# A hybrid attention block with a seven-product MLP: first pieces of a second product prepared behind the last evictions, and VectorE in the source's order

## The chip, the cores and the metric

The kernel runs on one NeuronCore of a Trainium2 chip. The metric is the device time in microseconds (us) of one execution. A core has five engines that run their own instruction streams side by side: TensorE (PE; its weight loads are listed as PEld), VectorE (DVE), ScalarE (ACT), GpSimd (POOL) and SyncE (SP), which here only issues DMA transfers. Each engine takes its instructions strictly in the order in which they stand in its stream, so an instruction that waits holds up everything behind it on the same engine. TensorE accumulates into PSUM banks; the other engines read those ("evict" them) and write to SBUF.

## The reference

One layer of a streaming encoder, 1024 tokens by 1024 features, all in float32:

```
n = rms_norm(x, g1);  proj = n @ w_in
y = [mixer_a(...) , mixer_b(...)]        # two attention groups, each normalised
h = x + concat(y) @ w_out
m = rms_norm(h, g2)
h = h + (relu(m @ w_ff1) ** 2) @ w_ff2   # 1024 -> 4096 -> 1024
out = rms_norm(h, final_g)
```

The change touches the MLP's two products and the work around them, the last third of the time.

## The kernel before, in words

**Seven products for eight.** Both MLP products are done by a Strassen-like scheme: a product of 2x2 blocks of 512 by 512 takes seven block products, with sums and differences of blocks as operands, and each block product takes three TensorE passes over float16 halves (a high part and the rest, the low part). An operand is thus first a float32 tile, then a high part (ScalarE copies it to float16, L1410) and a low part (tile minus high part: GpSimd L1412, or VectorE L1414).

**First product.** The 4096 hidden features come in eight slices n = 0..7. For each slice `product1(n, p)` runs p = 1, 5, 6, 3, 7, 2, 4 (list `order1`); 24 matmuls of 128x512 each. Products 1, 6, 7 and 4 accumulate in one PSUM pair (in the order's names `f1_n_1`), products 5 and 3 in a second, product 2 in a third, so TensorE can begin product 4 only when product 7 has been evicted. ScalarE evicts products 1, 5 and 6 to tiles k; VectorE evicts products 3, 7 and 2 (a custom operation at L1473 adds the PSUM pair to a k tile and takes a row maximum into `topf`, then L1475 squares the positive part). For product 4, ScalarE does relu and square, VectorE a row maximum (L1471), and then come four block sums on VectorE (L1484 to L1490). Every finished block goes by `put` to DRAM (`ud`), seven per slice, on SP's queue in order.

**Second product.** The slices go in four groups g of GQ = 2. `order2` lists pieces (g, p, n): for each product p both slices n of the group accumulate in one pair of PSUM tiles (chain a, b or c). A piece is 24 matmuls. `prepare2(at)` makes the operands of piece `at`, AHEAD2 = 2 pieces ahead of use: U is the block that `load2u` has read back from `ud` (LOAD2 = 6 pieces ahead, SP queue), scaled by ScalarE (L1408) and split (ScalarE L1410, GpSimd L1412; for p = 5 VectorE instead of GpSimd); V is a block of the second weights or a difference Z of such blocks (VectorE L1384), split by ScalarE L1410 and VectorE L1414. After both slices of a product, `add_up` (VectorE, L1733) adds the PSUM tiles to result blocks C, once per half and in some products for two blocks.

The first four pieces, group 0's products 1 and 5, are prepared inside the loop of the first product:

```
FIRST_PIECES = {(7, 1): 0, (7, 5): 1, (7, 6): 2, (7, 3): 3}
...
        if (n, p) in FIRST_PIECES:
            prepare2(FIRST_PIECES[n, p])
```

**The end.** In the last group the order of products is 1, 2, 5, 6, 3, 7, 4. Token blocks 0 to 3 are complete after product 3; their final norms (`final`, generators that are stepped) are issued behind product 7: squares on ScalarE (L1747), small columns and reciprocals on VectorE (L1777, L1779), the scaling on GpSimd and VectorE, and the copy of the gains (L1825). Product 4, which finishes blocks 4 to 7, runs in row pieces (`last_product`), each followed by the norm of its block.

**What sets the order.** A scheduler with a timeline of its own orders each engine's instructions; source order is only its input. The class `InOrder` (L159) wraps an engine so that each of its instructions depends on the one before it in the source, which pins the order; such an instruction has L159 as its line. In the kernel before, SP's queue is pinned in the MLP, ScalarE is pinned in the first product from its ninth step on, TensorE is pinned throughout, and VectorE and ScalarE are pinned in the last product. `dve` is the plain VectorE (L508).

Of the kernel before, what the change touches and what calls it, by code (L numbers as in the profile page):

```python
# [13 lines left out]
ALU = mybir.AluOpType  # L14
# [10 lines left out]
NQ = DFF // (4 * P)  # L25
# [9 lines left out]
GQ = 2  # L35
# [10 lines left out]
}  # L46
FIRST_PIECES = {(7, 1): 0, (7, 5): 1, (7, 6): 2, (7, 3): 3}
START_FILL = 3
A_FILL = 7
B_FILL = [13, 13, 9.5, 9.5] * 2 + [11.25] * 8  # L50
# [15 lines left out]
def kernel(  # L66
# [29 lines left out]
    nc = tc.nc  # L96
# [411 lines left out]
    dve, pool = nc.vector, nc.gpsimd  # L508
# [630 lines left out]
    def flat(t):  # L1139
        return t.rearrange("p a b -> p (a b)")  # L1140
# [278 lines left out]
    def prepare1(n, p, at):  # L1419
        if n >= NQ or (n, p) in wops:  # L1420
            return
        made = wsum.setdefault(n, {})
        if n:
            scaled1(n, *{1: ((0, 0), (0, 1)), 5: ((0, 1), (1, 1)), 6: ((1, 1), (1, 0))}.get(p, ((1, 0), (0, 1), (1, 1))))
        second = page2 if at < 2 or at > 4 else page1
        t = second_operands(
            lambda i, j: w1s[n, i, j], made, p, f"T{n}_{p}", dve, lambda name: second([P, 4, 2 * P], name)
        )
        wops[n, p] = split(
            t, f"W{n}_{p}", dve if at < 7 and at != 2 else pool, lambda name: page16([P, 2, 4, 2 * P], name), None if n else to_scale1[0][0]  # L1430
        )
# [3 lines left out]
    def product1(n, p):  # L1435
        a, c = chains.setdefault(n, [None, None])
        if p in (1, 5, 2):
            ps = pair_psum(f"f1_{n}_{p}")
            if p == 1:
                chains[n][0] = ps  # L1440
            if p == 5:
                chains[n][1] = ps
        else:
            ps = c if p == 3 else a
        hi, lo = wops.pop((n, p))
        for u in range(2):
            cols = slice(u * P, (u + 1) * P)
            for k in range(4):
                x2 = [X[p][k // 2][:, hl, k % 2] for hl in range(2)]
                mm3(ps[:, u], (hi[:, k, cols], lo[:, k, cols]), x2, k == 0 and p in (1, 5, 2), k == 3, True)  # L1450
                if k % 2:
                    turn()
        while stores:
            stores.pop(0)()
        kept = saved.setdefault(n, {})
        ps = flat(ps)
        if p in (1, 5, 6):
            if p == 5 and n:
                kept[p] = tst([P, 2 * HALF], f"k{n}_{p}")
            else:  # L1460
                kept[p] = page2([P, 2 * HALF], f"k{n}_{p}")
            act1[0].activation(kept[p], ps, AF.Copy)
            return
        v = tst([P, 2 * HALF], f"v{n}") if p == 4 else kept[{3: 6, 7: 5, 2: 1}[p]]
        if n not in topf:
            topf[n] = small.tile([P, 4], F32, tag="topf", bufs=2, name=f"topf_{n}")
        top = topf[n][:, {3: 0, 7: 1, 2: 2, 4: 3}[p] :][:, :1]
        if p == 4:
            act1[0].activation(v, ps, AF.Relu)
            act1[0].activation(v, v, AF.Square)  # L1470
            dve.tensor_reduce(top, ps, mybir.AxisListType.X, ALU.max)  # L1471
        else:
            dve.tensor_tensor_reduce(v, ps, v, 1.0, 0.0, ALU.add, ALU.max, top)  # L1473
            if n:
                dve.scalar_tensor_tensor(v, v, 0.0, v, ALU.max, ALU.mult)  # L1475
            else:
                act1[0].activation(v, v, AF.Relu)
                act1[0].activation(v, v, AF.Square)
        if p != 4:
            put(n, {3: 2, 7: 4, 2: 1}[p], v)  # L1480
            return

        u00, u01, u11, u10 = kept[1], kept[6], kept[5], v
        dve.tensor_tensor(u11, u10, u11, ALU.add)  # L1484
        put(n, 5, u11)
        dve.tensor_tensor(u10, u00, u10, ALU.subtract)
        put(n, 7, u10)
        dve.tensor_tensor(u00, u11, u00, ALU.subtract)
        put(n, 6, u00)
        dve.tensor_tensor(u01, u01, u00, ALU.subtract)  # L1490
        put(n, 3, u01)
        if n % GQ == 0:
            topu[n // GQ] = Top(f"u{n // GQ}", NQ + n // GQ, GQ)
        top, col = topf.pop(n), topu[n // GQ].column()
        nc.vector.tensor_reduce(col, top, mybir.AxisListType.X, ALU.max)
        nc.vector.tensor_tensor(col, col, down1[n], ALU.mult)
        if n % GQ == GQ - 1:
            topu[n // GQ].gather()
# [138 lines left out]
    def prepare2(at):  # L1637
        if at >= len(order2) or order2[at][1:] in ready2:
            return
        g, p, n = order2[at]  # L1640
        ready2.add((p, n))
        alloc = page if at <= 3 * GQ else page3
        high = lambda name: page16([P, 2, 2, HALF], name, alloc)
        temp = lambda name: alloc([P, 2, HALF], name, F32)
        a = u2s.pop((n, p))
        b = second_operands(lambda i, j: w2s[n, i, j], made_b.setdefault(n, {}), p, f"Z{n}_{p}", dve, temp)
        ops2[n, p] = (
            split(a, f"U{n}_{p}", dve if p == 5 else pool, high, uup[n]), split(b, f"V{n}_{p}", dve, high, up2[g])
        )

    queue[0] = InOrder(nc.sync)
    for at, (n, p) in enumerate(order1):
        if at == 8:
            act1[0] = InOrder(nc.scalar)
        if p == (1 if n > 1 else 5) and n:
            load1(n + 1)
        ahead1 = at + (AHEAD1 + 1 if at < AT_ONCE else AHEAD1)

        behind = (n, p) == (0, 2)
        if ahead1 < len(order1) and not behind:  # L1660
            prepare1(*order1[ahead1], ahead1)
        product1(n, p)
        for work in chores.get((n, p), ()):
            combined(*work)
            if behind and work[0] == 5:
                prepare1(*order1[ahead1], ahead1)
        if 0 < n < NQ - 1:
            if p == 3:
                see1(n + 1)
            if p == 7:  # L1670
                scale1(n + 1)
        if p == 3 and n and n % GQ == 0:
            scale_of_u(n // GQ - 1)
        if at > 6:
            look2(at, p != 1)
        for i, blocks in FIRST_LOADS.get((n, p), ()):
            if i is not None:
                fetch2(i)
            for tile2 in blocks:
                load2w(*tile2)  # L1680
        if (n, p) in FIRST_PIECES:
            prepare2(FIRST_PIECES[n, p])
    assert not to_see and not on_way and not to_scale
    act1[0] = nc.scalar
    acc = {}
# [44 lines left out]
    def add_up(p, q2):  # L1730
        ps = banks["a" if p in (1, 6, 7, 4) else "b" if p == 2 else "c"][q2]
        c = acc[(*into[p], q2)]
        nc.vector.scalar_tensor_tensor(flat(c), flat(ps), down2[g], flat(c), ALU.mult, ALU.add)  # L1733

    def final(tb, dve, act, first=None):

# [64 lines left out]
    for at, (g, p, n) in enumerate(order2[:-GQ]):  # L1801
        fetch2(at + LOAD2)
        step = at % (7 * GQ)
        if g + 1 < NQ // GQ:
            if step in range(4, 12):
                load2w(*blocks2(g + 1)[step - 4])
        if step == 1:
            scale_sums(g)
        if g + 1 == NQ // GQ and step == 2:
            down, up = down2[g], scale_tile("up", "", 1)  # L1810
            nc.vector.reciprocal(up, down)
        if g == 0 and step in (4, 7, 10):
            last = NQ // GQ - 1
            {4: topu[last].write, 7: topu[last].read, 10: lambda: scale_of_u(last, False)}[step]()
        prepare2(at + AHEAD2)
        if at in (1, 3, 9):
            load_acc(*into[{1: 5, 3: 6, 9: 4}[at]])
        if at == 6:
            queue[0].dma_start(gfb, final_g.partition_broadcast(P))
        if product2(g, p, n):  # L1820
            for q2 in range(2):
                add_up(p, q2)
        if (g, p) == (NQ // GQ - 1, 3) and n % GQ == GQ - 1:
            gains.append(fps.tile([P, D], F32, tag=f"{'ab'[1 ^ g % 2]}0", bufs=1, name="gains"))
            nc.scalar.activation(gains[0], gfb, AF.Copy)  # L1825
        if (g, p) == (NQ // GQ - 1, 7):
            if n % GQ == GQ - 1:
                h = acc[1, 0, 1][:, 1]
                nc.vector.scalar_tensor_tensor(h, banks["a"][1][:, 1], down, h, ALU.mult, ALU.add)
            two = [final(2 * (n % GQ) + b, dve, nc.scalar) for b in range(2)]  # L1830
            for _ in range(4):
                for work in two:
                    next(work)

    g, p, n0 = order2[-GQ]
    in_order = InOrder(nc.vector), InOrder(nc.scalar)

# [102 lines left out]
```

## Time and profile before

| what | value |
|---|---|
| three runs | 1033.74, 1030.7, 1032.37 us; median 1032.37 |
| the profiled execution: its own time | 1034.48 us |
| the profiled execution: span from first to last instruction | 1032.7 us |
| mean granted TensorE clock | 0.994 |
| DMA moved | 200.63 MB, mean 194 GB/s |
| U tiles read back from `ud` | 56 transfers of 512 KB, median 5.7 us from issue to landing |
| results stored to `ud` | 48 transfers of 512 KB in that group, 3.6 us |

Times in the views are microseconds from the start of the span. In a timeline a row is: start, busy time, engine, line, operation, out<-in, partitions x elements and type, count, and in brackets the idle time ahead of it on that engine and what ended it. A wait row is: engine, what waits, line, `<-` what released it, then total us, times, longest. In the rows of windows: the stretch, its length, then busy time (and instructions) of PE, PEld, DVE, ACT and POOL, the granted TensorE clock, the busy share of DMA and GB/s. Busy shares are averages over stages with different limits, and the profiled execution is 2.1 us above the median of the three runs, so differences are taken against its own span.

### The profile page before, as it was taken

How to read it: one execution, taken by the hardware profiler on the slowest of the kernel's cores; microseconds unless marked ns; L12 is line 12 of the kernel's file. 1: busy time of each engine (PE TensorE's matmuls, PEld its weight loads, DVE VectorE, ACT ScalarE, POOL GpSimd, SP SyncE). 2: the span in 40 equal slices, each digit the busy share in tenths (PEclk: the TensorE clock that was granted, in tenths of full speed). 3: DMA queues.
4: the chain of work that ended last, by engine and by line, in shares of the span. 5: the costliest groups of instructions: out<-in, count | busy, mean ns of one | idle time of the engine just before them, and what ended most of it. 6: DMA issues, size and time to landing. Idle time of an engine off the chain costs nothing. (4 is left out here: it accounts for less than half of the span.)

```text
span 1032.7 us, 14046 instructions
## 1 busy us (share of the span) xinstructions
PE 997.6 (97%) x4818; PEld 590.7 (57%) x4818; DVE 805.6 (78%) x1288; ACT 650.5 (63%) x1060; POOL 448.9 (43%) x341
## 2 busy tenths in 40 slices
PE   9999999999979999989999999999899999999997
PEld 7888887777756668644444444444344444444443
DVE  5576787867675738995989999979886887686976
ACT  8676766766576745676646655756286655557446
POOL 0466665242452472106335444446163243345333
PEclk9999999999989999999999999999999999999999
DMA  9944527999999894205778668738699454443004
GB/s 355 267 126 130 139 77 186 192 211 228 211 248 225 201 304 159 86 21 183 252 257 285 218 228 288 248 141 304 223 299 401 142 181 137 169 162 123 1 1 163
DMA packets 150567, 200.63 MB, mean 194 GB/s; under 512 B 78688, under 2 KB 96224, under 8 KB 150496
## 3 DMA queue, kind: packets, MB, share of 16 engines
q1 hardware_dynamic: 150352, 199.47, 64.0%
q8 instruction: 38, 0.62, 0.3%
q14 instruction: 33, 0.27, 0.1%
q10 hardware_dynamic: 144, 0.26, 0.1%
HBM read 120.01 MB, written 42.99 MB: 158 GB/s over the span
## 5 line engine op out<-in xcount | busy, mean ns | idle before, releaser
L179 PE MATMUL f<-X,W 128*128 128x512 f16 x1344 | 294.5, 381 | 6.2 <-DVE topf L1473 3.9
L179 PEld LDWEIGHTS <-W 128*128 128x128 f16 x1344 | 131.6, 98 | 164.0 <-issue 7.5
L179 PEld LDWEIGHTS <-U 128*128 128x128 f16 x1356 | 132.4, 98 | 160.6 <-ACT V L1410 1.8
L1412 POOL TENSOR_TENSOR U<-u,U 128x1024 f16<-128x1024 f32 x48 | 120.9, 2531 | 167.7 <-ACT U L1410 157.3
L179 PE MATMUL f_a<-V,U 128*128 128x512 f16 x756 | 165.3, 379 | 0.9 <-DVE C L1733 0.9
L1412 POOL TENSOR_TENSOR W<-T,W 128x1024 f16<-128x1024 f32 x29 | 73.4, 2532 | 82.6 <-ACT W L159 49.4
L1412 POOL TENSOR_TENSOR W<-w,W 128x1024 f16<-128x1024 f32 x21 | 49.4, 2353 | 90.1 <-ACT W L159 69.2
L1408 ACT ACTIVATE u<-u,uupn 128x1024 f32<-128x1024 f32 x46 | 52.1, 1144 | 56.2 <-DMA u<-ud 55.3
L179 PE MATMUL f_c<-V,U 128*128 128x512 f16 x384 | 84.2, 379 | 1.4 <-DVE C L1733 1.4
L1414 DVE SCALAR_TENSOR_TENSOR V<-Z,up,V 128x1024 f16<-128x1024 f32 x32 | 52.3, 1638 | 28.2 <-ACT V L1410 23.3
L631 ACT ACTIVATE P_B<-P_B,nm_B 128x640 f32<-128x640 f32 (+2 forms) x64 | 44.2, 691 | 32.0 <-DVE nm_B L628 16.5
L1410 ACT ACTIVATE U<-u 128x1024 f16<-128x1024 f32 x46 | 48.1, 1045 | 25.6 <-DVE Z L1384 11.3
L179 PE MATMUL op_A<-w_o,y 128*128 128x512 f32 x192 | 58.6, 430 | 5.7 <-DVE ts_vB L441 5.1
L876 DVE SCALAR_TENSOR_TENSOR H_B<-P_B,rc_B,H_B 128x640 f16<-128x640 f32 (+2 forms) x64 | 50.8, 822 | 13.7 <-ACT H_B L871 13.3
L179 PE MATMUL ip_qB<-nT,w_qB 128*128 128x512 f32 x192 | 53.8, 406 | 1.1 <-DVE t_kB L415 1.0
L1414 DVE SCALAR_TENSOR_TENSOR V<-w,up,V 128x1024 f16<-128x1024 f32 x24 | 42.9, 1791 | 14.8 <-ACT V L1410 7.8
L179 PE MATMUL ip_kB<-nT,w_kB 128*128 128x512 f32 x192 | 53.7, 405 | 0.0
L179 PE MATMUL ip_vB<-nT,w_vB 128*128 128x512 f32 x192 | 51.3, 400 | 0.0
L159 ACT ACTIVATE w<-w,up 128x1024 f32<-128x1024 f32 x24 | 26.7, 1137 | 38.5 <-DVE up L1162 38.5
L179 PE MATMUL ip_qA<-nT,w_qA 128*128 128x512 f32 x192 | 50.5, 397 | 0.3 <-DVE VA L185 0.3
L1410 ACT ACTIVATE V<-Z,up 128x1024 f16<-128x1024 f32 x30 | 34.1, 1137 | 25.4 <-DVE Z L1384 24.8
L871 ACT ACTIVATE H_B<-P_B,rc_B 128x640 f16<-128x640 f32 (+2 forms) x64 | 40.8, 685 | 9.9 <-DVE rc_B L868 4.5
(295 smaller groups left out, 2007.1 us busy)
## 6 DMA issues: line engine op xcount, KB each, us to landing
w<-in_w_ff_dram SPq DMA_DIRECT2D x64, 512.0 KB, 7.2
u<-ud SPq DMA_DIRECT2D x56, 512.0 KB, 5.7
ud<-k SPq DMA_DIRECT2D x48, 512.0 KB, 3.6
m<-in_w_ff_dram SPq DMA_DIRECT2D x32, 512.0 KB, 5.9
KkB<-t_kB SPq DMA_DIRECT2D x32, 256.0 KB, 5.1
xr<-in_x_dram SPq DMA_DIRECT2D x8, 512.0 KB, 9.2
st_o<-in_w_out_dram SPq DMA_DIRECT2D x8, 512.0 KB, 4.3
h<-in_x_dram SPq DMA_DIRECT2D x8, 512.0 KB, 4.9
```

The lines of the kernel that those rows point to most:

```text
L159: ins = getattr(self.engine, op)(*args, **kw)
L179: pe(nc.tensor.matmul(*args, **kw))
L631: nc.scalar.activation(pr, pr, AF.Exp, bias=nm, scale=-1.0, accum_out=sm)
L871: nc.scalar.activation(hi, q, AF.Copy, scale=rc)
L876: nc.vector.scalar_tensor_tensor(lo, q, rc, hi, ALU.mult, ALU.subtract)
L1408: act1[0].activation(full, full, AF.Copy, scale=up)
L1410: act1[0].activation(w[0], full, AF.Copy, scale=1.0 if up is None else up)
L1412: engine.tensor_tensor(w[1], full, w[0], ALU.subtract)
L1414: engine.scalar_tensor_tensor(w[1], full, up, w[0], ALU.mult, ALU.subtract)
```

## The change

Pieces 2 and 3 (group 0's product 5) are prepared two products later in the source, behind the evictions of products 2 and 4 of slice 7. The sums that end slice 7 move into a function `finish1`, called behind the last of these pieces. From product 7 of slice 7 until the last product, `dve` is an `InOrder` VectorE, and `add_up` goes through it. The final norms of blocks 0 to 3 use the plain VectorE as before (they were passed `dve` and are now passed `nc.vector`).

```
-FIRST_PIECES = {(7, 1): 0, (7, 5): 1, (7, 6): 2, (7, 3): 3}
+FIRST_PIECES = {(7, 1): 0, (7, 5): 1, (7, 2): 2, (7, 4): 3}
@@ product1
+        last_sums.append(lambda: finish1(n, kept, v))
+        if n < NQ - 1:
+            last_sums.pop()()
+
+    last_sums = []
+
+    def finish1(n, kept, v):
+
         u00, u01, u11, u10 = kept[1], kept[6], kept[5], v
         dve.tensor_tensor(u11, u10, u11, ALU.add)
@@ loop over order1
+        if (n, p) == (NQ - 1, 7):
+            dve = InOrder(nc.vector)
         product1(n, p)
...
         if (n, p) in FIRST_PIECES:
             prepare2(FIRST_PIECES[n, p])
+        if (n, p) == (NQ - 1, 4):
+            last_sums.pop()()
@@ add_up
-        nc.vector.scalar_tensor_tensor(flat(c), flat(ps), down2[g], flat(c), ALU.mult, ALU.add)
+        dve.scalar_tensor_tensor(flat(c), flat(ps), down2[g], flat(c), ALU.mult, ALU.add)
@@ loop over order2
-            two = [final(2 * (n % GQ) + b, dve, nc.scalar) for b in range(2)]
+            two = [final(2 * (n % GQ) + b, nc.vector, nc.scalar) for b in range(2)]
...
+    dve = nc.vector
     g, p, n0 = order2[-GQ]
     in_order = InOrder(nc.vector), InOrder(nc.scalar)
```

The orders of TensorE and SP stay as they were. Those of VectorE, ScalarE and GpSimd move, at three places above all. In the rows, `k7_5` is the tile that product 7 of slice 7 is evicted to, `k7_6` that of product 3, `k7_1` that of product 2; `Z0_5` or `U1_5` are operands of slice 0's or 1's product 5.

VectorE at the end of the first product, before:

```order
L1384 TENSOR_TENSOR Z0_5_7053<-w2_0_01_6946,w2_0_00_6901 128x1024
L1414 SCALAR_TENSOR_TENSOR V1_1_7013<-w2_1_00_6905,up2_0_5795,V1_1_7013 128x1024
L1384 TENSOR_TENSOR Z1_5_7091<-w2_1_01_6950,w2_1_00_6905 128x1024
L1414 SCALAR_TENSOR_TENSOR U0_5_7055<-u0_5_6944,uupn_0_5570,U0_5_7055 128x1024
L1473 ISA k7_6_7045,topf_7_7088<-f1_7_5_6962,k7_6_7045 128x1024
L1473 ISA topf_7_7088 128x1
L1414 SCALAR_TENSOR_TENSOR V0_5_7058<-Z0_5_7053,up2_0_5795,V0_5_7058 128x1024
L1475 SCALAR_TENSOR_TENSOR k7_6_7045<-k7_6_7045 128x1024
L1414 SCALAR_TENSOR_TENSOR U1_5_7093<-u1_5_6948,uupn_1_5572,U1_5_7093 128x1024
L1414 SCALAR_TENSOR_TENSOR V1_5_7096<-Z1_5_7091,up2_0_5795,V1_5_7096 128x1024
L1473 ISA k7_5_6987,topf_7_7088<-f1_7_1_6913,k7_5_6987 128x1024
```

and the same place now:

```order
L1414 SCALAR_TENSOR_TENSOR V1_1_7013<-w2_1_00_6905,up2_0_5795,V1_1_7013 128x1024
L1473 ISA k7_6_7045,topf_7_7080<-f1_7_5_6962,k7_6_7045 128x1024
L1473 ISA topf_7_7080 128x1
L1475 SCALAR_TENSOR_TENSOR k7_6_7045<-k7_6_7045 128x1024
L159 ISA k7_5_6987,topf_7_7080<-f1_7_1_6913,k7_5_6987 128x1024
L159 ISA topf_7_7080 128x1
L159 SCALAR_TENSOR_TENSOR k7_5_6987<-k7_5_6987 128x1024
L159 ISA k7_1_6942,topf_7_7080<-f1_7_2_7115,k7_1_6942 128x1024
L159 ISA topf_7_7080 128x1
L159 SCALAR_TENSOR_TENSOR k7_1_6942<-k7_1_6942 128x1024
L159 TENSOR_TENSOR Z0_5_7143<-w2_0_01_6946,w2_0_00_6901 128x1024
L159 SCALAR_TENSOR_TENSOR U0_5_7145<-u0_5_6944,uupn_0_5570,U0_5_7145 128x1024
```

The six operations of product 5 (Z, U, V of slices 0 and 1) stood ahead of the eviction of product 7 and now stand behind those of products 7 and 2; behind them come V0_5, the row maximum of product 4, Z1_5, U1_5, V1_5 and then the four sums. On ScalarE, the high parts for product 5 stood ahead of those of the weights of products 2 and 4 of slice 7 and now stand behind them.

ScalarE at group 0's product 7, where `u0_7` is a U tile to be scaled and `U0_7` its high part, before:

```order
L1408 ACTIVATE u0_7_7277<-u0_7_7277,uupn_0_5570 128x1024
L1408 ACTIVATE u1_7_7312<-u1_7_7312,uupn_1_5572 128x1024
L1410 ACTIVATE U0_7_7432<-u0_7_7277 128x1024
L1410 ACTIVATE V0_7_7436<-Z0_7_7430,up2_0_5795 128x1024
L1410 ACTIVATE U1_7_7472<-u1_7_7312 128x1024
L1410 ACTIVATE V1_7_7476<-Z1_7_7470,up2_0_5795 128x1024
L1408 ACTIVATE u0_2_7353<-u0_2_7353,uupn_0_5570 128x1024
L1408 ACTIVATE u1_2_7389<-u1_2_7389,uupn_1_5572 128x1024
```

and now:

```order
L1408 ACTIVATE u0_7_7277<-u0_7_7277,uupn_0_5570 128x1024
L1408 ACTIVATE u1_7_7312<-u1_7_7312,uupn_1_5572 128x1024
L1408 ACTIVATE u0_2_7353<-u0_2_7353,uupn_0_5570 128x1024
L1408 ACTIVATE u1_2_7389<-u1_2_7389,uupn_1_5572 128x1024
L1408 ACTIVATE u0_4_7426<-u0_4_7426,uupn_0_5570 128x1024
L1410 ACTIVATE U0_7_7432<-u0_7_7277 128x1024
L1410 ACTIVATE V0_7_7436<-Z0_7_7430,up2_0_5795 128x1024
L1410 ACTIVATE U1_7_7472<-u1_7_7312 128x1024
```

Three scalings of later products' tiles, u0_4's the last of them, have moved ahead of product 7's high parts; u0_4 stood behind the high parts of product 2.

VectorE ahead of the last product, where `C010` and `C011` are halves of the result block that product 3 completes, `qf`, `wf`, `rf` and `fo` belong to the norms of token blocks 0 to 3, and `V7_4` is an operand of the last product, before:

```order
L1384 TENSOR_TENSOR Z7_4_9203<-w2_7_10_8663,Z7_6_8953 128x1024
L1414 SCALAR_TENSOR_TENSOR V6_4_9132<-Z6_4_9126,up2_3_6999,V6_4_9132 128x1024
L1414 SCALAR_TENSOR_TENSOR V7_4_9209<-Z7_4_9203,up2_3_6999,V7_4_9209 128x1024
L1733 SCALAR_TENSOR_TENSOR C010_7323<-f2_3_c_0_8925,down2_3_8805,C010_7323 128x1024
L1733 SCALAR_TENSOR_TENSOR C011_7325<-f2_3_c_1_8926,down2_3_8805,C011_7325 128x1024
```

and now:

```order
L1789 RECIPROCAL qf_3_9253<-uf_3_9251 128x1
L1791 RECIPROCAL rf_0_9163<-wf_0_9161 128x1
L1790 TENSOR_SCALAR wf_2_9241<-wf_2_9241,qf_2_9242,uf_2_9240 128x1
L1791 RECIPROCAL rf_1_9174<-wf_1_9172 128x1
L1790 TENSOR_SCALAR wf_3_9252<-wf_3_9252,qf_3_9253,uf_3_9251 128x1
L1799 SCALAR_TENSOR_TENSOR fo_0_9159<-C000_7196,rf_0_9163,gains_9124 128x512
L1791 RECIPROCAL rf_2_9243<-wf_2_9241 128x1
L1799 SCALAR_TENSOR_TENSOR fo_1_9170<-C000_7196,rf_1_9174,gains_9124 128x512
L1791 RECIPROCAL rf_3_9254<-wf_3_9252 128x1
L159 SCALAR_TENSOR_TENSOR V7_4_9209<-Z7_4_9203,up2_3_6999,V7_4_9209 128x1024
L159 SCALAR_TENSOR_TENSOR C110_7247<-f2_3_a_0_8777,down2_3_8805,C110_7247 128x1024
```

V7_4 stood ahead of C010 and of all the norms of blocks 0 to 3, and now stands behind their reciprocals; C010 and C011 (rows of product 3) stand ahead of Z6_4 and V6_4 now, where they stood behind V7_4. On ScalarE the squares of the norms, which stood behind the high parts of U and V for the last product, are now mixed in between these high parts.

At one more place, between products 2 and 5 of the last group, VectorE had the additions of product 2 to C000 and C001 behind Z7_6, V6_6 and V7_6 (operands of product 6); they now stand directly behind V7_5.

## The prediction

> **What bounds the kernel now.** The page's first two lines say where to look.
>
> ```profile
> span 1032.7 us, 14046 instructions
> PE 997.6 (97%) x4818; PEld 590.7 (57%) x4818; DVE 805.6 (78%) x1288; ACT 650.5 (63%) x1060; POOL 448.9 (43%) x341
> ```
>
> TensorE is busy for 97% of the span and the change adds no matmul, so only two things can move the time: TensorE's idle gaps and the clock behind a gap. Next, TensorE's waits from 700 us on, all four of them, and the rows of its timeline where they lie.
>
> ```profile
> PE f L179 <- DVE topf L1473: 3.9, 1, 3.9
> PE f L179 <- POOL W L1412: 1.7, 1, 1.7
> PE f_c L179 <- DVE C L1733: 1.4, 1, 1.4
> PE f_a L179 <- DVE C L1733: 0.9, 1, 0.9
> ```
>
> ```profile
> 717.99 4.92 PE L179 MATMUL f<-X,W 128*128 128x512 f16 x22 [1.74 <-POOL W L1412]
> ...
> 726.81 6.91 PE L179 MATMUL f<-X,W 128*128 128x512 f16 x24 [3.90 <-DVE topf L1473]
> 733.56 10.52 PE L179 MATMUL f_a<-V,U 128*128 128x512 f16 x48
> ...
> 775.00 10.52 PE L179 MATMUL f_a<-V,U 128*128 128x512 f16 x48
> ...
> 1004.45 10.52 PE L179 MATMUL f_a<-V,U 128*128 128x512 f16 x48
> 1015.93 7.93 PE L179 MATMUL f_a<-V,U 128*128 128x512 f16 x36 [0.95 <-DVE C L1733]
> ```
>
> The row at 726.81 is slice 7's product 4. 24 matmuls took 6.91 us there; at the rate of the rows of 48 (10.52) they take 5.18 from start to start, so 1.73 us were lost. A window shows why (the number before the last two is the granted clock):
>
> ```profile
> 726.80:730.20 3.40, 3.39 (x9) 1.23 (x9) 3.37 (x4) 0.00 (x0) 0.00 (x0) 0.53 0.38 154
> ```
>
> After 3.90 us idle the clock stood at 0.53 for 3.4 us. The rows at 775.00 (group 0's product 7) and 1004.45 (the last group's product 7) have no gap now.
>
> **Step 1, the end of the first product: a gain.** Why the two gaps ahead of 733.56 exist is in the other engines' timelines:
>
> ```profile
> 714.38 1.04 ACT L159 ACTIVATE W<-w 128x1024 f16<-128x1024 f32 x1
> 715.50 2.43 POOL L1412 TENSOR_TENSOR W<-w,W 128x1024 f16<-128x1024 f32 x1 [5.79 <-ACT W L159]
> 725.54 1.21 DVE L1473 CUSTOM_DVE_ANT_0 k<-f,k 128x1024 f32<-128x1024 f32 x1
> ```
>
> Product 2's weight was split late, since ScalarE's high part (714.38) stood behind product 5's; now product 5's stand behind it, and the 1.74 go. The eviction of product 7 ran at 725.54, although product 7 had ended before 717.99: the six operations for product 5 that stood around it on VectorE ran first, without a pause, as VectorE's own window shows (busy 11.00 of 11.00 us; the clock behind 1.74 us idle stayed at 1.00):
>
> ```profile
> 715.00:726.00 11.00, 11.00 (x9) 1.00 0.72 280
> ```
>
> Now none stands ahead of it. It lies beside product 2's 5.18 us, so the 3.90 go, and with the gap the slow clock, 1.73. Sum −7.37: the second product would start at 726.19 instead of 733.56. What hides the moved operations is the first pieces of group 0: product 1 runs 10.36 us ahead of product 5. Bounds: −7.4, and −5.6 if the weight of product 2 is no earlier (it also waits for GpSimd); I take −7.37, because nothing is left on ScalarE ahead of it.
>
> **Step 2, group 0's product 7: a new wait.** The six operations come after product 2 now, and the four sums behind them. The last of the sums before:
>
> ```profile
> 741.53 1.22 DVE L1490 TENSOR_TENSOR k<-k,k 128x1024 f32<-128x1024 f32 x1
> ```
>
> Product 2 of slice 7 ends at about 721.2 (717.99 − 1.74 + 4.92). Then VectorE has nine operations (two for the eviction, three each for slices 0 and 1, the maximum) of 1.2 to 1.3, 11.2 in all, then four sums, 4.9, and one wait of about 2.1 for an operand that GpSimd holds: 739.4, where it was 742.75. So the last sum is 3.4 us earlier, not 7.4. SP takes its queue in order: its loads of U stand behind the store of that sum. The fifth, of u0_4, matters:
>
> ```profile
> 756.03 0.32 SPq L159 DMA_DIRECT2D u<-ud  x1
> u<-ud SPq DMA_DIRECT2D x1, 512.0 KB, 14.1
> 771.25 1.14 ACT L1408 ACTIVATE u<-u,uupn 128x1024 f32<-128x1024 f32 x1
> ```
>
> It was issued at 756.03 and landed 14.1 later, at 770.1; its scaling ran at 771.25 and cost nothing, since product 7's high parts stood ahead of it on ScalarE. Now u0_4's scaling stands ahead of product 7's high parts, and they wait for its landing, at 766.7 if it moves with the sums. Behind it:
>
> ```profile
> 984.90 1.13 ACT L1410 ACTIVATE V<-Z,up 128x1024 f16<-128x1024 f32 x1
> 985.07 2.13 POOL L1412 TENSOR_TENSOR U<-u,U 128x1024 f16<-128x1024 f32 x1 [8.73 <-ACT U L1410]
> 986.06 2.21 DVE L1414 SCALAR_TENSOR_TENSOR V<-Z,up,V 128x1024 f16<-128x1024 f32 x1 [0.84 <-ACT V L1410]
> 988.31 1.23 DVE L1384 TENSOR_TENSOR Z<-w,w 128x1024 f32<-128x1024 f32 x1
> ...
> 998.84 1.27 DVE L1414 SCALAR_TENSOR_TENSOR V<-Z,up,V 128x1024 f16<-128x1024 f32 x1
> ```
>
> Scaling 1.14, U's high part 1.04 (as the copy at 714.38), its low part on GpSimd 2.13, V's low part 1.27 (it took 2.21 beside GpSimd, so it counts behind it): 5.5, so product 7 has its operands at 772.2. TensorE gets there at 775.00 − 7.37 = 767.63. That is +4.6. For the second slice GpSimd's U1_7 (2.13), then Z (1.23), V's high part (1.13) and low part (1.27) follow one another, to about 778.0, where TensorE would want it at 772.81: +5.2; I take +5.1, since TensorE can begin on the high parts alone. Bounds: 0 if the load lands by 762.1 (767.63 − 5.5), +8.5 if it lands no earlier than now (770.1).
>
> The Trainium skill, SBUF — State Buffer, section "Who interferes with whom", says that VectorE and GpSimd share one pair of ports as an exclusive lock. The trace agrees: 2.21 beside GpSimd, 1.27 alone. By it VectorE and GpSimd would follow each other as I added them.
>
> **Step 3, between products 2 and 5 of the last group: a small gain.** The 1.38 gap is this:
>
> ```profile
> 969.82 2.22 DVE L1414 SCALAR_TENSOR_TENSOR V<-Z,up,V 128x1024 f16<-128x1024 f32 x1 [1.08 <-ACT V L1410]
> 971.96 2.46 DVE L1733 SCALAR_TENSOR_TENSOR C<-f_b,down,C 128x1024 f32<-128x1024 f32 x2
> ```
>
> The additions of product 2 free the bank that TensorE waits for; they stood behind V7_6 (969.82), which waits for ScalarE. In source order they come before product 6's operands: −1.4. Bounds 0 and −1.4; I take the latter, since nothing late is left ahead of them.
>
> **Step 4, ahead of the last product: a loss.** With E for the start of the last group's product 7 (1004.45), the last product began at E + 11.48 (1015.93). Rows that price the new order on ScalarE and VectorE:
>
> ```profile
> 1003.21 1.27 DVE L1733 SCALAR_TENSOR_TENSOR C<-f_c,down,C 128x1024 f32<-128x1024 f32 x1
> 1004.52 1.03 ACT L1825 ACTIVATE gains<-gfb 128x1024 f32<-128x1024 f32 x1 [3.23 <-DVE C L1733]
> 1005.48 0.61 ACT L1747 ACTIVATE fo<-C 128x512 f32<-128x512 f32 x1
> ```
>
> and a window of VectorE alone over the reciprocals of blocks 0 to 3, first to last:
>
> ```profile
> 1010.08:1013.30 3.22, 3.04 (x17) 1.00 0.21 78
> ```
>
> Product 3's additions to C010 (1003.21 was the first of two) now begin behind V7_7, at about E + 0.3. First one: 1.3. Then ScalarE: the gains 1.0, four squares 2.4, a high part 1.0, two squares 1.2, V6_4's high part 1.1: E + 8.3. VectorE: V6_4's low part 1.3, Z7_4 1.2: E + 10.8. Then the small columns and reciprocals in a row, 3.2, with V7_4 behind them: 1.3, and behind that the addition to C110 that frees the bank for the last product: 1.3, to E + 16.5. So +5.0. TensorE then idles for about 6 us; 3.90 cost a slow clock, so I add 1.73 once more. Bounds: +3.5 without the clock, if C010 runs as early as now (−1.24 from E), and +8.2 with further waits for GpSimd (two of 0.7).
>
> **Step 5, the rest at nothing.** Between the two, VectorE in source order is covered by its slack:
>
> ```profile
> 775.00:1004.40 229.40, 228.02 (x1057) 103.15 (x1056) 176.91 (x131) 129.60 (x123) 92.54 (x38) 1.00 0.42 147
> ```
>
> VectorE is busy 177 of 229 us, ScalarE 130. If the cover is gone, each product's operands are late by what one instruction waits; that is the fourth rival.
>
> **Sum.** −7.4 + 5.1 − 1.4 + 5.0 + 1.7 = +3.1 us on a span of 1032.7. The profiled execution (1034.48) is 2.1 above the median of the runs, 1032.37; on the median the sum gives 1035.5. About 0.3% (3.1 us) is what a measurement of this kernel can tell from no change.
>
> **The rivals.**
>
> (a) Not slower: u0_4's load lands by 762.1, and step 2's wait is absent. For it: the median of the kernel's U loads is far under 14.1, as this line of issues shows for the stretch behind the sums.
>
> ```profile
> u<-ud SPq DMA_DIRECT2D x8, 512.0 KB, 9.7
> ```
>
> Issued at 752.6 (3.4 earlier) with 9.7, it lands at 762.3, at the point of decision. Against: it was the slowest of these loads, and the same other transfers stand around it. 3.1 − 5.1 = −2.0: 1030.4. Chance 0.18.
>
> (b) The tail is shorter: C010 as early as now, 1.5 less: 1034.0. For it: the additions wait only for product 3; against: V7_7 waits for ScalarE. Chance 0.10.
>
> (c) The clock falls at group 0's product 7 too. Its wait is in two parts, about 2.4 us for V's high part, two matmuls, 1.9 for the low part. The 1.74 us at 717.99 cost no clock, the 3.90 did, and two matmuls are little work between. The price is 1.7: 1037.2. Chance 0.16. The Trainium skill, TensorE: Matmul & The Clock Gate, section "What's actually happening", says that the clock is halved after about one idle window of 3.4 us, in windows that run free of the program; by that a broken gap of 4.3 may or may not halve it. The trace has no such broken gap.
>
> (d) VectorE in source order bounds the steps of product 5 in each group. VectorE has two additions to C and six operations of about 1.25 there (Z, U and V of two slices), 10 us of the 10.36 that TensorE takes; one wait for ScalarE (1.08 and 0.84 in the rows at 969.82 and 986.06) is passed on. Three further groups at 1 to 2 us: +3 to +6 on the sum, 1038.5 to 1041.5. Against: operands are made two pieces, 10 us, ahead, which absorbs single waits. Chance 0.11.
>
> **How the numbers follow.** The forecast, all five steps as walked, has 0.45, and 1035.5 is its time; its own range is 1033.5 to 1037.5 (bounds of steps 2 and 4). The range of all cases runs from 1029.5, (a) with half a microsecond off the other steps' losses, to 1039.5, (d) with its nearer end: under 0.1 is left out on each side. Slower by over 0.3% is above 1035.5: half of the forecast, (c) and (d): 0.50. Within it: the other half, (b), and most of (a): 0.39. Faster, under 1029.3: the part of (a) where step 4 comes out near its lower bound as well: 0.11.
>
> **What the profile after would show.** Right: no gap in TensorE ahead of slice 7's products 2 and 4, and the second product's first row at about 726.2; at group 0's product 7 (about 767.6) two gaps released by ScalarE and VectorE (V or U), ScalarE's scaling of u ahead of them ended by a DMA; no gap at product 5 of the last group; a gap of about 6 us ahead of the last product, released by VectorE's C, with a granted clock near 0.53 behind it. Wrong would be: a second product that starts no earlier, u0_4 landed before 762, gaps in groups 1 and 2 (d), or a tail gap under 3 us, which would take 3 to 5 us off the sum.

## The result, and the profile after

The changed kernel takes 1037.84 us (five runs, 1036.25 to 1040.03), the kernel before 1032.01 in the same comparison: a ratio of 1.0057, interval 1.0042 to 1.0072, or 4 to 7 us slower. The forecast was 1035.5, in a range of 1029.5 to 1039.5, with slower as the likeliest case.

The first lines of the page after:

```profile
span 1034.5 us, 14031 instructions
PE 999.8 (97%) x4818; PEld 592.0 (57%) x4818; DVE 814.5 (79%) x1288; ACT 649.8 (63%) x1060; POOL 446.0 (43%) x341
```

TensorE's waits behind 600 us, all three:

```profile
PE f_a L179 <- DVE C L159: 7.7, 1, 7.7
PE f_a L179 <- DVE V L159: 2.7, 4, 1.9
PE f_a L179 <- ACT V L1410: 0.2, 1, 0.2
```

Both waits of the first product (3.9 and 1.7) and the one of the last group (1.4) are gone. One of 7.7 us has come ahead of the last product, and a broken one at product 7. TensorE's timeline says where:

```profile
698.28 0.27 PE L182 MATMUL all_w<-ident,top_w 128*128 128x128 f32 x1
698.39 26.06 PE L179 MATMUL f<-X,W 128*128 128x512 f16 x120
724.29 10.52 PE L179 MATMUL f_a<-V,U 128*128 128x512 f16 x48
...
766.08 0.38 PE L179 MATMUL f_a<-V,U 128*128 128x512 f16 x1 [0.19 <-ACT V L1410]
768.33 5.34 PE L179 MATMUL f_a<-V,U 128*128 128x512 f16 x24 [1.87 <-DVE V L159]
773.90 5.12 PE L179 MATMUL f_a<-V,U 128*128 128x512 f16 x23 [0.23 <-DVE V L159]
778.86 10.52 PE L179 MATMUL f_b<-V,U 128*128 128x512 f16 x48
...
997.32 10.52 PE L179 MATMUL f_a<-V,U 128*128 128x512 f16 x48
1015.58 10.05 PE L179 MATMUL f_a<-V,U 128*128 128x512 f16 x36 [7.74 <-DVE C L159]
```

The row of `all_w`, a small transpose in the middle of slice 7, is a good mark, since nothing ahead of it moved. In the profile before it stands here:

```profile
700.00 0.27 PE L182 MATMUL all_w<-ident,top_w 128*128 128x128 f32 x1
```

That is 1.7 us later for the same work; over all profiles of this study the mark lies between 696.89 and 700.61. So the two spans (1032.7 and 1034.5) can't be compared as they are, but the stretches behind the mark can:

| stretch | before, us | after, us | forecast | measured |
|---|---|---|---|---|
| mark to the second product's start | 33.56 | 26.01 | −7.4 | −7.55 |
| from there to group 0's product 2 (product 7 has its wait in it) | 51.80 | 54.57 | +5.1 | +2.77 |
| to the last group's product 7 | 219.09 | 218.46 | −1.4 | −0.63 |
| to the last product's start | 11.48 | 18.26 | +5.0 | +6.78 |
| to the end | 16.77 | 18.92 | +1.7 | +2.15 |
| sum | 332.7 | 336.2 | +3.1 | +3.5 |

(Before, group 0's product 2 begins at 775.00 + 10.36 = 785.36.) The runs say 2 us more than this profile; the experiments show a part of these.

### The profile page after: what moved, and what is told of

Its sections match the earlier page's. It is cut to its first block, busy times and chain, and to the rows that moved or that the text cites. A ratio compares the mean times of both kernels' runs of the same rounds, so it can differ in the third digit from the quotient of the medians.

```text
span 1034.5 us, 14031 instructions
## 1 busy us (share of the span) xinstructions
PE 999.8 (97%) x4818; PEld 592.0 (57%) x4818; DVE 814.5 (79%) x1288; ACT 649.8 (63%) x1060; POOL 446.0 (43%) x341
## 4 chain that ended last, share of the span: by engine, by line
PE 50%; DMA 6%; DVE 5%; ACT 3%; issue 1%; SPq 0%; DVEq 0%; ACTq 0%
PE f L179 27%; PE f_a L179 10%; PE f_c L179 5%; PE f_b L179 3%; PE op_B L179 3%; DMA w<-in_w_ff_dram 2%; DMA u<-ud 2%; DVE V L159 1%; DVE Z L159 1%; DMA C<-hB 1%; DMA G_B<-H_B 1%; ACT V L1410 1%; DVE h L1250 1%; ACT U L1410 1%; PE op_A L179 0%
## 5 line engine op out<-in xcount | busy, mean ns | idle before, releaser
L1412 POOL TENSOR_TENSOR U<-u,U 128x1024 f16<-128x1024 f32 x48 | 114.6, 2400 | 178.1 <-ACT U L1410 161.0
L179 PE MATMUL f_a<-V,U 128*128 128x512 f16 x756 | 168.1, 382 | 10.6 <-DVE C L159 7.7
L159 DVE SCALAR_TENSOR_TENSOR V<-Z,up,V 128x1024 f16<-128x1024 f32 x32 | 46.1, 1440 | 39.8 <-ACT V L1410 39.6
L159 DVE SCALAR_TENSOR_TENSOR C<-f_a,down,C 128x1024 f32<-128x1024 f32 (+1 forms) x32 | 39.2, 1243 | 12.5 <-PE f_a L179 12.4
L179 PE MATMUL S_B<-KkB,QqB 128*128 128x320 f32 (+2 forms) x192 | 41.9, 328 | 5.2 <-DVE nm_B L628 3.7
```

The lines of the kernel that those rows point to most:

```text
L159: ins = getattr(self.engine, op)(*args, **kw)
L179: pe(nc.tensor.matmul(*args, **kw))
L1412: engine.tensor_tensor(w[1], full, w[0], ALU.subtract)
```

## The experiments

All are edits of the changed kernel unless another is named; each has five rounds against the kernel before on the same chip. "From the mark" is the span's end minus the row of `all_w`: 332.7 before, 336.2 in the changed kernel. The first theory had two parts: the head gains 7.5 us by the moved pieces, and VectorE's source order loses more at two places behind.

**1. Only the head: VectorE pinned in the first product alone.**

```
     act1[0] = nc.scalar
+    dve = nc.vector
     acc = {}
```

> The changed kernel with VectorE pinned to source order in the first product alone; the second product goes in the scheduler's order, where u0_4's scaling stands behind product 7's high parts. Theory (two independent parts: the head gains 7.5 us, the pinned second product loses it again): no gap ahead of products 2 and 4 of slice 7, none at group 0's product 7, the 1.4 us gap of the last group is back, 1024 to 1026. Rival (group 0's product 7 waits because the loads behind the sums come late for a second product that starts 7 us earlier, whatever the order): a gap of 2 to 3 us stays at product 7, 1027 to 1029.

1023.24 us against 1030.84, ratio 0.9928 (0.9913 to 0.9943): as the theory had it, and faster than both kernels. From the mark 324.4. All of TensorE's waits from 690 us on:

```profile
PE f_a L179 <- DVE C L1746: 0.9, 1, 0.9
PE f_c L179 <- DVE C L1746: 0.5, 1, 0.5
```

The rival falls: u0_4's load is issued 25.3 us behind the second product's start, as in the changed kernel (25.35), so it is no earlier, and product 7 doesn't wait. Its high parts stand ahead of u0_4's scaling.

**2. Only the order: the pieces of product 5 where they were.**

```
-FIRST_PIECES = {(7, 1): 0, (7, 5): 1, (7, 2): 2, (7, 4): 3}
+FIRST_PIECES = {(7, 1): 0, (7, 5): 1, (7, 6): 2, (7, 3): 3}
```

> The changed kernel with the first pieces of product 5 where they were before, so VectorE in source order is all that is left of the change. Theory (the head's gain is all from the moved pieces, the tail's loss all from the order): the gaps of 1.7 and 3.9 us ahead of products 2 and 4 of slice 7 are as before, the tail waits about 7 us, group 0's product 7 waits under 1 us since TensorE comes there 7 us later than in the changed kernel; before plus 8 to 10: 1040 to 1042. Rival (the order costs only together with the early start of the second product): 1031 to 1034.

1040.00 us, ratio 1.0086 (1.0069 to 1.0103).

```profile
PE f_a L179 <- DVE C L159: 7.7, 1, 7.7
PE f L179 <- DVE topf L159: 3.9, 1, 3.9
PE f L179 <- POOL W L1412: 1.4, 1, 1.4
```

The head's waits are back, the tail's 7.7 us are there in full, and product 7 has no wait. (In `order1` the two pieces move by three products; the section on the change says two.) With 1 and 2 the change comes apart: the moved pieces, with the pin in the first product, give 7.6 us; the order takes about 9 without them. The two don't add up to the change: −7.6 and +9.2 make +1.6, and the change costs 5.8. Most of the difference is the wait at group 0's product 7 with its slow clock (priced in 10), which neither of these two kernels has.

**3. The pieces moved, no pin at all** (`dve = InOrder(nc.vector)` left out).

> The changed kernel without the pinned VectorE: the pieces of product 5 and the last sums are moved in the source, and the scheduler sets VectorE's order, in which U0_5 and V0_5 stay ahead of the eviction of product 7. Theory (the head's gain is the eviction's place on VectorE, so the pin is needed for it): the 1.7 us gap ahead of product 2 is gone, one of 2 to 3.5 us ahead of product 4 stays, and the second product is as in the kernel with the first product alone pinned, so 1025 to 1029. Rival (moving the pieces in the source is enough): no gap, 1023.

1028.98 us, ratio 0.9979 (0.9970 to 0.9988). The eviction of product 7 stays behind U0_5 and V0_5:

```profile
722.15 7.03 PE L179 MATMUL f<-X,W 128*128 128x512 f16 x24 [3.08 <-DVE topf L1473]
```

3.08 us of wait, and the 24 matmuls behind it take 7.03 instead of 5.18. The pin in the first product is worth the other 5 us; moving the pieces in the source alone gives 2.

**4. ScalarE pinned too, through the second product.**

```
-    act1[0] = nc.scalar
     acc = {}
```

> The changed kernel with ScalarE pinned to source order through the second product as well, so that product 7's high parts stand ahead of the scaling of u0_2, u1_2 and u0_4. Theory (the wait at group 0's product 7 is u0_4's load, passed on by ScalarE's order): no gap there, the tail's 7.7 us stay, so 2.8 us under the changed kernel: 1034 to 1036. Rival (the operands of product 7 are late by their own loads and by GpSimd): the gap of 2.3 us stays, 1037 to 1039.

1032.21 us, ratio 1.0021 (1.0006 to 1.0036): by the ratios 4 to 5 us under the changed kernel, more than expected. The wait at product 7's first slice is gone, so it was u0_4's load, passed on by ScalarE; 0.86 us stay at the second slice (the cause is in 9), the clock behind it is 1.00, and the tail waits 5.6 instead of 7.7, which was not expected.

```profile
PE f_a L179 <- DVE C L159: 5.6, 1, 5.6
PE f_a L179 <- DVE V L159: 0.9, 1, 0.9
```

**5. VectorE plain from the last product's operands on.**

```
+        if order2[at + AHEAD2][:2] == (NQ // GQ - 1, 4):
+            dve = nc.vector
         prepare2(at + AHEAD2)
```

> The changed kernel with one edit: VectorE is plain again from the operands of the last product on, so V7_4 and the addition to C110 stand ahead of the norms of token blocks 0 to 3. Theory (the end of the second product pays 6.8 us of added wait and 2.1 us of slow clock because V7_4 stands behind those norms): the last product starts within 1.5 us of the end of product 7, the clock behind it is 1.00, and the time is 8.9 us under the changed kernel's 1037.8, so 1027 to 1030. Rival (product 3's additions to C, and not the order behind them, are late): the wait of about 7.7 us stays, 1036 to 1039.

1033.55 us, ratio 1.0021 (1.0007 to 1.0036): by the ratios 4 to 5 us less, where 8.9 were expected. V7_4 now runs ahead of the norms, but the wait only halves:

```profile
1013.09 10.63 PE L179 MATMUL f_a<-V,U 128*128 128x512 f16 x36 [3.51 <-DVE C L1745]
```

Here the addition to C110 stands behind the norms instead (it ran at 1011.67 on VectorE, though product 7 ended before 1009.6), and the slow clock stays. So the theory of the tail was half of it, which led to 6 and 7.

**6. The norms of blocks 0 to 3 behind product 7's additions, on the pinned VectorE.**

```
-        if (g, p) == (NQ // GQ - 1, 7):
-            if n % GQ == GQ - 1:
-                h = acc[1, 0, 1][:, 1]
-                nc.vector.scalar_tensor_tensor(h, banks["a"][1][:, 1], down, h, ALU.mult, ALU.add)
-            two = [final(2 * (n % GQ) + b, nc.vector, nc.scalar) for b in range(2)]
+        if (g, p, n % GQ) == (NQ // GQ - 1, 7, GQ - 1):
+            h = acc[1, 0, 1][:, 1]
+            dve.scalar_tensor_tensor(h, banks["a"][1][:, 1], down, h, ALU.mult, ALU.add)
+            four = [final(tb, dve, nc.scalar) for tb in range(2 * GQ)]
```

> The changed kernel with the norms of token blocks 0 to 3 issued on the pinned VectorE behind product 7's additions, so V7_4 and the additions to C110 and C111 stand ahead of them; C010 and C011 stay where the change put them. Theory (the tail waits because V7_4 and C110 stand behind the norms): the wait ahead of the last product falls from 7.7 to 1 to 3 us, too short for a slow clock, and the time is 6 to 8 us under the changed kernel's 1037.8: 1029.5 to 1032. Rival (C010's additions behind V7_7 make everything late, whatever stands behind them): a wait of 5 us or more stays, 1035 to 1038.

1039.34 us, ratio 1.0081 (1.0067 to 1.0095): a miss, and the rival's sign, a wait of 5 us or more, is there. With nothing of the norms ahead of V7_4 and C110 on VectorE the last product still waits 6.84 us. VectorE's own waits show what is first in line (V6_4's low part):

```profile
1007.77 2.30 DVE L159 SCALAR_TENSOR_TENSOR V<-Z,up,V 128x1024 f16<-128x1024 f32 x1 [4.46 <-ACT V L1410]
1010.00 2.28 DVE L159 TENSOR_TENSOR Z<-w,Z 128x1024 f32<-128x1024 f32 x1
1013.55 1.78 DVE L159 SCALAR_TENSOR_TENSOR V<-Z,up,V 128x1024 f16<-128x1024 f32 x1 [1.28 <-ACT V L1410]
```

It waits 4.46 us for its high part on ScalarE, which stands behind the gains and six squares there. The theory of the tail was changed: ScalarE's order is the first link.

**7. As 6, and ScalarE in source order from the last product's operands on.**

```
+        if order2[at + AHEAD2] == (NQ // GQ - 1, 4, NQ - GQ):
+            act1[0] = InOrder(nc.scalar)
...
-            four = [final(tb, dve, nc.scalar) for tb in range(2 * GQ)]
+            four = [final(tb, dve, act1[0]) for tb in range(2 * GQ)]
```

> The kernel with the norms behind product 7's additions on VectorE, and one edit more: ScalarE goes in source order from the last product's operands on, so that the high parts for the last product stand ahead of the squares of blocks 0 to 3. Theory (second form: the tail waits because V6_4's high part stands behind C010, the gains and six squares on ScalarE, and everything of the last product behind V6_4): the wait ahead of the last product falls from 6.8 to 1 to 2 us and its 36 matmuls take 7.9 us; the norms come later instead, which may cost 1 to 4 us at the end: 1029 to 1034. Rival (GpSimd's share of the ports, which stretched V6_4, Z7_4 and V7_4 from 1.25 to about 2.2 us): a wait of 5 us or more stays, 1036 to 1040.

1035.16 us, ratio 1.0042 (1.0030 to 1.0055), 4 us under 6. The wait ahead of the last product fell from 6.84 to 2.08, close to what the second form of the theory said, but the time lies above the expected 1029 to 1034: the norms are late inside the last product instead, which takes 23.3 us to the end of the span where it took 16.8 before the change:

```profile
1012.86 7.03 PE L179 MATMUL f_a<-V,U 128*128 128x512 f16 x24 [2.08 <-ACT fo L159]
1021.64 2.75 PE L179 MATMUL f_a<-V,U 128*128 128x512 f16 x12 [1.76 <-DVE f_a L159]
1024.23 1.47 PE L179 MATMUL end<-V,U 128*128 128x256 f16 x12
1027.46 1.47 PE L179 MATMUL end<-V,U 128*128 128x256 f16 x12 [1.75 <-ACT end L159]
```

The expected 7.9 us for 36 matmuls was a miss: the first 24 took 7.03 behind only 2.08 us of idle time. The additions to C010 begin 0.38 us behind product 7's start in 6 and in 7, so the rival of 6 (their lateness alone) falls. GpSimd has a part: V6_4's low part and Z7_4 take 1.85 and 1.21 us here, and 2.30 and 2.28 in 6, 1.5 of the 4.8 us.

**8. The tail's wait filled with 27 matmuls of zeros** into a spare PSUM tile.

```
+    spare = fps.tile([P, HALF], F32, tag=f"{'ab'[1 ^ g % 2]}1", bufs=1, name="spare")
+    for m in range(27):
+        matmul(spare, zero.to_broadcast([P, P]), zero.to_broadcast([P, HALF]), start=m == 0, stop=m == 26)
```

> The changed kernel with 27 matmuls of zeros into a spare PSUM tile between product 7 and the last product, some 6 us of work inside the wait of 7.7 us; their results are not read. Theory (the 2.1 us that the last product's 36 matmuls take longer are a slow clock behind idle time): the last product starts when it did, its 36 matmuls take 7.9 us instead of 10.05, the granted clock is 1.00 there, 1.5 to 2.5 us under the changed kernel: 1035.3 to 1036.3. Rival (the matmuls are slow because their operands or banks come piece by piece): they still take about 10 us, 1037 to 1039.

1035.28 us, ratio 1.0048 (1.0035 to 1.0061), about 2 under the changed kernel's 1037.27 on the same chip. No wait was shortened; only the clock held:

```profile
1010.24 6.25 PE L179 MATMUL spare<-zero 128*128 128x512 f32 x27
1018.33 7.93 PE L179 MATMUL f_a<-V,U 128*128 128x512 f16 x36 [1.84 <-DVE C L159]
```

36 matmuls in 7.93 us, as before the change, where the changed kernel takes 10.05. Two microseconds of its loss are clock alone.

**9. Both places freed** (4 and 5 together), on two chips, and **the same with one instruction moved**.

```
-            nc.vector.tensor_reduce(top, self.all, mybir.AxisListType.X, ALU.max)
+            (dve if self.name == "u3" else nc.vector).tensor_reduce(top, self.all, mybir.AxisListType.X, ALU.max)
```

> The changed kernel with ScalarE in source order through the second product, and VectorE plain from the last product's operands on: the order of ScalarE puts product 7's high parts of group 0 ahead of u0_4's scaling, and the high parts of the last product ahead of most squares. Theory (the pinned VectorE costs at those two places alone): a wait of about 1 us at group 0's product 7 and of 1 to 2 us ahead of the last product, no slow clock, so 1024 to 1027. Rival (VectorE in source order costs something in every group): 1029 to 1033.

> The kernel with both places freed once more, on the same chip as the one with the moved maximum, for the comparison. Theory: 1026 to 1029, with a wait of 1 to 3.5 us at group 0's product 7 that ends with a VectorE instruction behind the maximum. Rival (the first runs were a chip's own): 1023 to 1025.

> The kernel with both places freed, with one instruction moved: the row maximum over all_u on VectorE, which waits for a DMA (all_u) and stood ahead of V1_7 of group 0's product 7, is put into the pinned order and so stands behind the pieces of product 2; nothing else moves on ScalarE, GpSimd, SyncE or TensorE. Theory (the 3.4 us that are left at product 7's second slice are that DMA, passed on by VectorE's order): no wait at product 7, 1023.5 to 1025.5, and runs that lie closer together than 1024.6 to 1031.8. Rival (V1_7 is late by its own operands): a wait of 1 us or more stays, 1026.5 to 1028.5.

Both freed: 1027.52 us, ratio 0.9969 (0.9954 to 0.9984), and on the second chip 1025.39, ratio 0.9945 (0.9925 to 0.9966), under the 1026 to 1029 expected there. The first lies half a microsecond above what was expected, because of one wait at product 7's second slice, 3.37 us in the first profile and 1.35 in the second. VectorE's timeline in the first:

```profile
759.36 1.22 DVE L159 TENSOR_TENSOR Z<-w,w 128x1024 f32<-128x1024 f32 x1
769.52 0.28 DVE L1204 TENSOR_REDUCE topall_u<-all_u 128x1 f32<-128x128 f32 x1 [8.95 <-DMA all_u<-top]
...
770.78 2.72 DVE L159 SCALAR_TENSOR_TENSOR V<-Z,up,V 128x1024 f16<-128x1024 f32 x1
```

V1_7's low part (770.78) had its operands, and stood behind a row maximum of 0.28 us that waits 8.95 us for a DMA; its value is needed in the last group. With the maximum behind it, the other four engines as they were:

```profile
762.02 1.86 DVE L159 SCALAR_TENSOR_TENSOR V<-Z,up,V 128x1024 f16<-128x1024 f32 x1 [1.22 <-ACT V L159]
```

V1_7 runs 8.8 us earlier, product 7 has no wait, and the time is 1024.58 us (1024.23 to 1025.92), ratio 0.9927 (0.9915 to 0.9939). The profiles show that the wait was that DMA; the runs alone don't, since this interval and that of the second chip's 1025.39 overlap. This kernel keeps VectorE pinned in all four groups up to the last product's operands, and by the ratios it is as good as the one with the pin in the first product alone. With ScalarE pinned too, VectorE's source order costs nothing in the groups themselves: from group 0's product 2 to the last group's product 7 TensorE takes 217.56 us, which is 42 pieces of 5.18, against 218.22 in experiment 1. What is left lies in the tail: from the last group's product 7 to the end it takes 2 us longer than before the change, with three waits (0.75, 0.35 and 1.57) inside the last product.

**10. The changed kernel once more.**

> The changed kernel once more, for a second profile and more runs. Theory (its waits at group 0's product 7 hang on when loads land, so they differ from run to run by one or two us): the wait at product 7 differs from the first profile's 2.3 us by more than 0.5, the wait ahead of the last product is 7 to 8.5 us, and the time is 1036 to 1040. Rival (the first runs were a chip's own): the time is within 2 us of the kernel before.

1037.27 us, ratio 1.0069 (1.0052 to 1.0086). The tail waits 7.7 us again. At product 7:

```profile
766.87 0.38 PE L179 MATMUL f_a<-V,U 128*128 128x512 f16 x1 [0.75 <-ACT V L1410]
769.11 11.63 PE L179 MATMUL f_a<-V,U 128*128 128x512 f16 x47 [1.87 <-DVE V L159]
```

The first part is 0.75 us (0.19 in the first profile), less of a difference than was expected; but in other profiles with the same order up to there it is 1.20 (experiment 5), 1.77 (6), 2.33 (7) and 0.25 (8), and the second part always 1.7 to 1.9. What differs most is what comes behind it. Windows over the first 3.4 us behind product 7's second wait (the granted clock is the number before the last two), in this profile:

```profile
769.11:772.50 3.39, 3.39 (x10) 1.30 (x10) 3.36 (x3) 1.32 (x2) 1.94 (x1) 0.60 1.05 406
```

and in the first profile of the changed kernel:

```profile
768.30:773.90 5.60, 5.34 (x24) 2.34 (x24) 5.50 (x10) 3.67 (x4) 2.31 (x2) 1.00 1.04 399
```

Ten matmuls in 3.39 us against 24 in 5.60. The clock fell at product 7 in all five other profiles with this order (0.50 to 0.60 over 3.4 us), and not in the first, which is the one compared above and the fastest of its five runs. In those five the 47 matmuls behind the wait take 11.6 to 12.4 us, and at the full rate (5.18 for 24) they would take 10.3, so the clock costs 1.3 to 2.1 us, which is most or all of the 2 us by which the runs exceed the first profile. Waits and clock together, from the second product's start to product 2, cost 2.77 us in the first profile and 4.1 to 6.6 in the five others.

## Why the prediction was right, and where it was off

**Step 1 (the head, −7.4) was right.** Measured −7.55, and 1 and 3 show that both halves are needed, the moved pieces and the eviction's place. The eviction of product 7 runs at 715.14 now:

```profile
715.14 1.21 DVE L159 CUSTOM_DVE_ANT_0 k<-f,k 128x1024 f32<-128x1024 f32 x1
```

**Step 2 (group 0's product 7, +5.1) had the mechanism, and for the profile compared above too large a size.** ScalarE's rows in the changed kernel:

```profile
760.30 1.15 ACT L1408 ACTIVATE u<-u,uupn 128x1024 f32<-128x1024 f32 x1 [5.52 <-DMA u<-ud]
762.90 1.15 ACT L1408 ACTIVATE u<-u,uupn 128x1024 f32<-128x1024 f32 x1 [1.45 <-DMA u<-ud]
763.95 1.04 ACT L1410 ACTIVATE U<-u 128x1024 f16<-128x1024 f32 x1
```

u0_4's scaling (762.90) waits for its load and product 7's high part follows, as forecast. The load landed 38.6 us behind the second product's start (762.90 − 724.29); the step had put 40.5 (766.7 − 726.19). With 38.6 the step gives 3.2, so in this profile that is the mis-sized term. It is not a fixed one: in the five other profiles with this order the load lands 38.7 to 40.8 us behind that start. The gap is in two parts with one matmul between, where the walk had two matmuls. Two readings behind the step were wrong without changing its sum: u0_4's load is the seventh behind the sums, not the fifth, and not the slowest of the eight (the one issued at 760.05 took 15.1).

**Step 3 (−1.4) was right, step 5 (the rest at nothing) nearly.** No wait at product 5 of the last group. Group 1's product 7 has two short waits now:

```profile
820.90 5.34 PE L179 MATMUL f_a<-V,U 128*128 128x512 f16 x24 [0.22 <-DVE V L159]
826.60 5.12 PE L179 MATMUL f_a<-V,U 128*128 128x512 f16 x23 [0.35 <-DVE V L159]
```

They are 0.6 us of idle time, and the table's stretch comes out 0.8 short of the 1.4. In experiment 10 that stretch lies 0.3 above its full rate (217.56), in 5 to 8 at it. Rival (d) falls: no profile with the pin in the second product has a wait at product 5 of groups 1 to 3, where (d) put them.

**Step 4 (the tail, +5.0 and +1.7) was right in its chain and short by 1.8 and 0.4.** VectorE there, with E = 997.32, then V6_4's high part on ScalarE and GpSimd's rows beside them:

```profile
997.70 2.47 DVE L159 SCALAR_TENSOR_TENSOR C<-f_c,down,C 128x1024 f32<-128x1024 f32 x2
...
1005.77 2.31 DVE L159 SCALAR_TENSOR_TENSOR V<-Z,up,V 128x1024 f16<-128x1024 f32 x1 [0.89 <-ACT V L1410]
1008.00 2.28 DVE L159 TENSOR_TENSOR Z<-w,Z 128x1024 f32<-128x1024 f32 x1
...
1012.98 1.26 DVE L159 SCALAR_TENSOR_TENSOR V<-Z,up,V 128x1024 f16<-128x1024 f32 x1
1014.17 2.46 DVE L159 SCALAR_TENSOR_TENSOR C<-f_a,down,C 128x1024 f32<-128x1024 f32 x2
...
1004.60 1.13 ACT L1410 ACTIVATE V<-Z,up 128x1024 f16<-128x1024 f32 x1
...
1005.70 3.49 POOL L1774 TENSOR_TENSOR fo<-C,gfb 128x512 f32<-128x512 f32 x2
1009.16 3.11 POOL L1412 TENSOR_TENSOR U<-u,U 128x1024 f16<-128x1024 f32 x1
```

C010 begins at E + 0.4 (forecast 0.3), V6_4's high part was ready at E + 8.4 (8.3). Then V6_4 and Z7_4 took 2.31 and 2.28 beside GpSimd, where the step had 1.3 and 1.2 alone: 2.1 us, the mis-sized term, named only as the upper bound. Experiments 6 and 7 add that ScalarE's squares, and not VectorE's reciprocals, are the first link: with the reciprocals gone from ahead of V7_4 the wait was still 6.84 us, with the squares gone too from ahead of the high parts it was 2.08.

**The sum.** The terms as written make 3.0; +3.1 is their unrounded sum. That it comes within half a microsecond of the profile's +3.5 is luck: step 2 was 2.3 too large there and the tail 2.2 too small. The runs, at 4 to 7 us slower, lie above the sum, inside the range. The range's ends were put 0.4 and 1 us beyond the cases that they were to stand for (1030.4 − 0.5 and 1038.5).

**The rivals.** (a) and (b) did not come. (c), a slow clock at product 7, came in five of the six profiles with this order, one of them the second profile of the changed kernel itself: it should have stood in the forecast. With its 1.3 to 2.1 us and the tail's 2.2, the sum would have been +4.3 to +5.1 even with step 2's smaller wait, inside the interval of the runs. **Open:** up to 2 us. The execution profiled in experiment 10 took 1037.30, by the median of its runs (1037.27), and has +4.3 behind the mark, where the runs say +6.0. The kernel before has one profile alone, of an execution 2 us above its median, so a part of the rest may lie there; no run shows it. The mean granted clock doesn't settle it: of the runs in experiment 10 one with 0.993 took 1037.30 and one with 0.988 took 1036.34.

## What to carry to other kernels

Pinning one engine to source order changes the orders of the others as well: look, for each of them, at what the scheduler now puts ahead of the critical operands. A cheap instruction that waits for a DMA (a scaling of 1.15 us, a maximum of 0.28 us) must stand behind every operand that is needed before its data land. Keep the part of a reorder that shortens the path (here the evictions, 7.6 us), and end the pin where it has done its work.

## What the runs showed of the hardware

The slow clock does not hang on the length of a gap alone. It followed 0.25 + 1.87 us with one matmul between, and 2.08 us ahead of the last product in experiment 7:

```profile
770.72:774.10 3.38, 3.38 (x9) 1.18 (x9) 3.35 (x3) 1.21 (x2) 1.93 (x1) 0.50 1.03 401
```

(this is the product 7 of experiment 8). In the first profile of the changed kernel nearly the same gap, 0.19 + 1.87 us, was followed by 1.00 (the row is in experiment 10), and 3.37 us without a matmul, in the first profile of experiment 9, by full clock too:

```profile
773.55:777.00 3.45, 3.45 (x16) 1.55 (x16) 3.45 (x3) 0.00 (x0) 0.00 (x0) 1.00 1.05 393
```

The Trainium skill, TensorE: Matmul & The Clock Gate, section "What's actually happening", says that activity is counted in windows of about 3.4 us that run free of the program. The runs agree in that gaps of equal length end either way. The slow stretches behind the gaps cost 1.3 to 2.7 us of matmul time in these profiles, which at a granted clock of 0.50 is 2.6 to 5.4 us (an estimate from these rows): of the order of such a window, and not exactly one. The Trainium skill, on the same page, section "Why this matters for your kernels", advises to keep gaps under about 3 us. That was not safe here: 2.1 us cost a slow stretch.
